# Narrow projection groups chained in PSUM, other terms for the wide ones, and weights and gate stores on other queues

## The chip, the cores and the metric

The kernel runs on one core of a Trainium2 chip as one launch. The metric is the device time of that launch in microseconds (us); the time before is the median of 3 runs.

## What is computed

One decoder layer on 2048 tokens of width 1024, in float32:

```
n    = RMSNorm(x)
proj = n @ w_in                      # split into gq, gk, gv, gr, glow, dq, dk, dv
o_a  = gated linear attention(gq, gk, gv, log_sigmoid(glow @ w2 + b) / 16)
o_a  = RMSNorm(o_a) * silu(gr)
o_b  = dilated sliding-window attention(dq, dk, dv), three branches, relative bias
h    = x + [o_a ; o_b] @ w_out
y    = RMSNorm(h + square(relu(RMSNorm(h) @ w_ff1)) @ w_ff2)
```

## The kernel before

**Stages.** The input projection takes the first 460 us, attention and the output projection follow to about 1040 us, then the first feed-forward product (FF1, to about 1690 us) and the second (FF2). Every large product is done by a Strassen-Winograd scheme of seven products instead of eight. Each factor is split into a high and a low part of 32 bits, and a product is three matmuls per piece (mm3, L139 to L142: L140 high by high, L141 low by high, L142 high by low). TensorE (PE) does nothing but these, transposes and the attention products.

**The projection.** The columns of w_in are nine groups (L249): dv, gr, dq, dk, dq, dk, gq, gk, gv. Two passes over the two halves of the tokens make 18 groups, g = 0 to 17. dv and gv are 256 columns wide on each of two sides n, gr 264 (the last 16 of its 512 + 16 are the low-rank gate); these are the wide groups. The other twelve are narrow, 128 columns a side. A group is seven products j in the order 1, 2, 5, 6, 3, 4, 7, one entry each of a list (jobs, L254). In a narrow product the combined weights stand in PE and 512 tokens stream past, twelve matmuls for the product; in a wide one the tokens stand and four token tiles take twelve matmuls each.

**What a product needs and leaves.** Two jobs ahead (L751), prep (L278) makes a product's weights: ScalarE (ACT) writes the high part wcomb (L288), VectorE (DVE) the low part (L290, or L292 with a scale for dq and gq), and DVE updates the sums of weights in place in the raw weights wraw (L294 to L300). Raw weights of the next group come from w_in by four loads (L271) on the queue of SyncE (SP), each issued when its quarter is free. A product's result stands in a bank of PSUM; the names ps_a, ps_c, ps_o, ps_d are kinds of bank, 2, 3, 1 and 2 of them, and bank() takes them in the turn a, c, a, o. rest() (L440 to L458) empties a bank: ACT copies products 1, 5 and 4 (L440, L445, L453), DVE adds products 2, 6, 3 and 7 (L442, L447, L450, L455) and adds three more times in SBUF (L448, L458 twice). So each group has seven DVE additions of results. The results stand in five halves of three slots called acc; c12 and c22 change places from group to group (L323).

**What is done with results.** finish (L329) sends them to DRAM: dq and dk are split again into high (L341, ACT) and low (L342, DVE) and stored by SP (L343). The gate group gr passes through log_sigmoid (L205 to L208), an exponential (L353), a product on DVE (L354), one on GpSimd (POOL, L355) and a store to srD by SP (L356); its last columns go to gate (L308), which transposes them (L315), multiplies them on PE (L318) and stores log gates to glD (L321, SP).

**FF1.** product1 (L1439) keeps its seven products in the order 1, 2, 6, 5, 7, 3, 4: products 1, 6, 7 and 4 go on accumulating in one bank, 5 and 3 in another, with a copy or an addition taken out between them. The weights w1raw come by GpSimd's queue (L1387), a group at a time in two halves, one for each half k of the rows.

**Order.** A list scheduler with a simulated timeline orders every engine's instructions when the kernel is built; the order of code is only its starting point. PSUM banks and SBUF slots are waited for by semaphores that the framework sets.

The functions that the diff touches:

Of the kernel before, what the change touches and what calls it, by code (L numbers as in the profile page):

```python
# [31 lines left out]
OTHER = [7, 9, 10, 11, 12, 13] + [14 * k + n for k in (1, 2, 3) for n in (0, 6, 10, 11, 12, 13)]  # L32
# [82 lines left out]
def emit(tc, a, stop=99):  # L115
# [137 lines left out]
    order = (1, 2, 5, 6, 3, 4, 7)  # L253
    jobs = [(g, j) for g in range(2 * NG) for j in order]  # L254
    w_in = a["w_in"].rearrange("o (c p) n -> p (o c) n", p=128)
    raws = [view(slot("wraw"), (2, 4, 264)) for _ in range(2)]
# [9 lines left out]

    def load_w(g, n, k):

        if g < 2 * NG:
            _, c0, w = groups[g % NG]  # L270
            SP.dma_start(raws[n][:, k, :, :w], w_in[:, 4 * k:4 * k + 4, c0 + n * w:c0 + n * w + w])  # L271
# [6 lines left out]
    def prep(at):  # L278
# [5 lines left out]
        (a11, a12), (a21, a22) = [[raws[n][:, k, :, :w] for k in range(2)] for n in range(2)]  # L284
        hi, lo = comb(at, w)
        src = {1: a11, 2: a12, 5: a21, 6: a21, 3: a12, 4: a22, 7: a21}[j]
# [8 lines left out]
        if j == 5:  # L295
            V.tensor_tensor(a21, a21, a11, op=OP.subtract)
            load_w(g + 1, 0, 0)
            V.tensor_tensor(a12, a12, a21, op=OP.subtract)
        if j == 6:
            V.tensor_tensor(a21, a22, a21, op=OP.subtract)  # L300
        if j == 3:
            load_w(g + 1, 0, 1)
        if j == 4:
            load_w(g + 1, 1, 1)
        if j == 7:
            load_w(g + 1, 1, 0)

    def gate(glow, t):  # L308
# [7 lines left out]
        V.tensor_copy(gT[:50], pt[:50, :128])  # L316
        pg = ps("d")[:, :256]
# [5 lines left out]
    def outputs(g):  # L323

        if g == 0:
            return c11, c12, c21, CX
        return (c11, (c12, c22)[g % 2], c21, (c22, c12)[g % 2])

    def finish(g, n, k, i):  # L329
# [4 lines left out]
        if w == 128:  # L334
# [5 lines left out]
            hi = c[:, 512:1024].bitcast(FR)  # L340
            A.activation(hi, c[:, :512], AF.Copy)  # L341
            V.tensor_tensor(c[:, :512], c[:, :512], hi.bitcast(F32), op=OP.subtract)  # L342
# [5 lines left out]
        if kind == "gr":  # L348
# [7 lines left out]
            SP.dma_start(srD[tk, j:j + m], s[:, :m])  # L356
# [11 lines left out]
    banks, held, late = [0], {}, []  # L368
# [31 lines left out]
    def product(at, i):  # L400
# [6 lines left out]
        if e == 0:  # L407
            held[j, i] = bank()
        p = held[j, i - e]
        B, W = TB[j], comb(at, w)  # L410
        n = w
        if w == 128:
            n = 512
            for c in range(4):
                mm3(p, W[0][:, c], W[1][:, c], B[0][:, c], B[1][:, c], c == 0, c == 3)
# [6 lines left out]
        def rest():  # L422
# [11 lines left out]
            def done(*which):  # L434
                for t in range(i - e, i + 1):
                    for n, k in which:
                        finish(g, n, k, t)

            if j == 1:
# [6 lines left out]
            elif j == 6:  # L446
                V.tensor_tensor(ix, q, ix, op=OP.add)  # L447
                V.tensor_tensor(c12, X, c22, op=OP.add)  # L448
            elif j == 3:
                V.tensor_tensor(i12, q, i12, op=OP.add)  # L450
                done((0, 1))
            elif j == 4:
                A.activation(i21, q, AF.Copy)  # L453
            else:
                V.tensor_tensor(ix, q, ix, op=OP.add)  # L455

                def sums(v, which, keep=lambda ins: None):
                    keep(V.tensor_tensor(v, v, X, op=OP.add))  # L458
                    done(which)

                for v, which in ((c21, (1, 0)), (c22, (1, 1))):
                    if at == len(jobs) - 1 and i == 3:
                        late.append((sums, v, which))
                    else:
                        sums(v, which)
# [3 lines left out]
    def bias_rows():  # L469

        rb, oh, rbo = xp[:33, :8], view(xp[:33, 8:], (3, 384)), view(bp[:8], (3, 384))
        SP.dma_start(rb[:32], a["rel_bias"])
        V.memset(rb[32:33], NEG)
        V.tensor_scalar(rb[:32], rb[:32], -1.0, None, op0=OP.mult)
        SP.dma_start(oh, a["c_onehot"])
        for d in range(3):
            p = ps("o")
            T.matmul(p[:8, :384], rb, oh[:, d], start=True, stop=True)
            V.tensor_copy(rbo[:, d], p[:8, :384])
        SP.dma_start(rowD, rbo)  # L480

# [14 lines left out]
    X = {}  # L496
# [1363 lines left out]
```

## Time and profile before

| | |
|---|---|
| runs | 2239.35, 2244.89, 2244.66 us, median 2244.66 |
| profiled execution | 2242.91 us, its span 2241.1 us (1.8 us lie around it) |
| PE busy | 2212.8 us (99%), 12420 matmuls |
| DVE busy | 1680.8 us (75%), 3173 instructions |
| ACT busy | 1253.5 us (56%), 2506 instructions |
| POOL busy | 533.6 us (24%), 535 instructions |

PE leaves 28.3 us of the span idle. A matmul's record runs on past the start of the next one, so PE's busy time is the union of records that overlap. Idle time of another engine costs nothing by itself.

### The profile page before, as it was taken

How to read it: one execution, taken by the hardware profiler on the slowest of the kernel's cores; microseconds unless marked ns; L12 is line 12 of the kernel's file. 1: busy time of each engine (PE TensorE's matmuls, PEld its weight loads, DVE VectorE, ACT ScalarE, POOL GpSimd, SP SyncE). 2: the span in 40 equal slices, each digit the busy share in tenths (PEclk: the TensorE clock that was granted, in tenths of full speed). 3: DMA queues.
4: the chain of work that ended last, by engine and by line, in shares of the span. 5: the costliest groups of instructions: out<-in, count | busy, mean ns of one | idle time of the engine just before them, and what ended most of it. 6: DMA issues, size and time to landing. Idle time of an engine off the chain costs nothing.

```text
span 2241.1 us, 35330 instructions
## 1 busy us (share of the span) xinstructions
PE 2212.8 (99%) x12420; PEld 1918.8 (86%) x12420; DVE 1680.8 (75%) x3173; ACT 1253.5 (56%) x2506; POOL 533.6 (24%) x535
## 2 busy tenths in 40 slices
PE   9999999999999999999999999999999999999998
PEld 8978998799999998887888888888888888888877
DVE  8787868666677677778777788777685697576798
ACT  7675446435787785555655566555555433333446
POOL 1110001016577673000000000000006222031462
PEclk9999999999999999999999999999999999999999
DMA  6467854787977877767744456555489988677775
GB/s 214 141 188 229 256 165 121 213 250 251 312 256 222 271 214 241 247 225 249 220 141 149 140 177 199 165 167 167 130 279 287 306 282 276 216 250 253 250 258 197
DMA packets 340934, 491.79 MB, mean 219 GB/s; under 512 B 20503, under 2 KB 237162, under 8 KB 330004
## 3 DMA queue, kind: packets, MB, share of 16 engines
q1 hardware_dynamic: 319842, 394.88, 54.6%
q0 software_dynamic: 13568, 41.95, 7.6%
q10 hardware_dynamic: 7346, 52.70, 6.3%
q8 instruction: 98, 1.61, 0.3%
q14 instruction: 80, 0.66, 0.1%
HBM read 335.52 MB, written 158.66 MB: 221 GB/s over the span
## 4 chain that ended last, share of the span: by engine, by line
PE 68%; issue 16%; DVE 7%; DMA 5%; POOL 2%; ACT 1%; SPq 0%; POOLq 0%; ACTq 0%; DVEq 0%
PE ps_a L141 7%; PE ps_a L142 6%; PE ps_a L140 6%; PE ps_c L141 5%; PE ps_c L142 5%; PE ps_c L140 5%; PE ps_a L909 4%; PE ps_d L141 3%; PE ps_d L142 3%; PE ps_d L140 3%; PE ps_o L141 3%; PE ps_o L140 3%; PE ps_o L142 3%; PE ps_d L890 3%; PE ps_c L872 2%
## 5 line engine op out<-in xcount | busy, mean ns | idle before, releaser
L490 ACT ACTIVATE cb<-bs 128x1024 fp32r<-128x1024 f32 x104 | 110.1, 1059 | 287.9 <-PE ps_o L141 94.6
L491 DVE TENSOR_TENSOR cb<-bs,cb 128x1024 fp32r<-128x1024 f32 x104 | 157.9, 1519 | 137.7 <-ACT cb L490 137.4
L1680 POOL TENSOR_TENSOR bs<-bs,rb 128x1024 f32<-128x1024 f32 x60 | 174.3, 2912 | 318.1 <-DMA bs<-w_ff 282.4
L491 DVE TENSOR_TENSOR w1comb<-w1raw,w1comb 128x512 fp32r<-128x512 f32 x224 | 153.2, 686 | 94.0 <-ACT w1comb L490 93.9
L1387 POOL DMA_DIRECT2D w1raw<-w_ff x64 | 48.2, 754 | 702.6 <-DVE w1comb L491 532.8
L490 ACT ACTIVATE w1comb<-w1raw 128x512 fp32r<-128x512 f32 x224 | 139.9, 627 | 92.0 <-PE ps_c L142 27.2
L881 ACT ACTIVATE pe<-pe,O 128x256 f32<-128x256 f32 (+1 forms) x384 | 157.5, 454 | 45.6 <-DVE O L880 41.9
L909 PE MATMUL ps_a<-v,pt 128*128 128x65 f32 x1200 | 180.8, 253 | 1.5 <-DVE pt L899 1.4
L909 PEld LDWEIGHTS ps_a<-v,pt 128*128 128x128 f32 x1200 | 175.7, 195 | 2.9 <-DVE pt L899 1.7
L880 DVE CUSTOM_DVE_ANT_0 pe<-ps_c,nb 128x256 f32<-128x256 f32 (+1 forms) x384 | 126.7, 360 | 46.8 <-PE ps_d L890 16.5
L890 PE MATMUL ps_d<-ident,pe 128*128 128x128 f32 x600 | 160.5, 281 | 0.0
L288 ACT ACTIVATE wcomb<-wraw 128x512 fp32r<-128x512 f32 (+2 forms) x119 | 90.1, 757 | 99.2 <-PE ps_a L141 33.0
L140 PE MATMUL ps_c<-hb,w1comb 128*128 128x512 f32 x320 | 124.6, 390 | 0.0
L141 PE MATMUL ps_c<-hb,w1comb 128*128 128x512 f32 x320 | 124.4, 389 | 0.0
L142 PE MATMUL ps_c<-hb,w1comb 128*128 128x512 f32 x320 | 124.1, 389 | 0.0
L491 DVE TENSOR_TENSOR ca<-ra,ca 128x1024 fp32r<-128x1024 f32 x84 | 121.8, 1451 | 0.1
L141 PE MATMUL ps_c<-cb,ca 128*128 128x512 f32 x312 | 121.5, 389 | 0.0
L140 PE MATMUL ps_c<-cb,ca 128*128 128x512 f32 x312 | 121.5, 389 | 0.0
L142 PE MATMUL ps_c<-cb,ca 128*128 128x512 f32 x312 | 121.4, 389 | 0.0
L890 PEld LDWEIGHTS ps_d<-ident,pe 128*128 128x128 f32 x600 | 109.2, 186 | 0.3
L355 POOL TENSOR_TENSOR acc<-acc,misc 128x264 f32<-128x264 f32 (+1 forms) x32 | 29.4, 924 | 319.3 <-DVE acc L354 303.9
L140 PE MATMUL ps_a<-wcomb,tb 128*128 128x256 f32 (+1 forms) x344 | 97.7, 284 | 0.0
(476 smaller groups left out, 7248.8 us busy)
## 6 DMA issues: line engine op xcount, KB each, us to landing
ra<-actD ACTq DMA_DIRECT2D x50, 1024.0 KB, 7.3
actD<-ring SPq DMA_DIRECT2D x176, 256.0 KB, 3.1
rb<-w_ff SPq DMA_DIRECT2D x88, 512.0 KB, 5.3
bs<-w_ff SPq DMA_DIRECT2D x72, 512.0 KB, 6.0
w1raw<-w_ff POOLq DMA_DIRECT2D x64, 512.0 KB, 5.3
k<-kD SPq DMA_DIRECT2D x16, 1024.0 KB, 7.9
rb<-hTD SPq DMA_DIRECT2D x28, 512.0 KB, 5.8
wraw<-w_in SPq DMA_DIRECT2D x48, 256.0 KB, 3.6
```

What stands on the lines that cost most here:

```text
L140: T.matmul(out, sh, mh, start=first, stop=False, **kw)
L141: T.matmul(out, sl, mh, start=False, stop=False, **kw)
L142: T.matmul(out, sh, ml, start=False, stop=last, **kw)
L288: A.activation(hi, src, AF.Copy, scale=sc)
L490: A.activation(hi, src, AF.Copy)
L491: V.tensor_tensor(lo, src, hi.bitcast(F32), op=OP.subtract)
L880: V.tensor_tensor_reduce(p, s, bias, scale=1.0, scalar=BIG, op0=OP.add, op1=OP.min, accum_out=nm)
L881: A.activation(p, p, AF.Exp, bias=nm, scale=-1.0)
L890: T.transpose(pb[:, i * 128:i * 128 + 128], src, ident)
L909: T.matmul(self.b.opsum[:, n % 4], self.pt[:, i * 128:i * 128 + 128], self.b.v[:, blk, cols], start=first, stop=last)
L1387: G.dma_start(raw1[g % 2][:, 4 * k:4 * k + 4], w1[:, 4 * k:4 * k + 4, g0:g0 + 256])
L1680: (engines or ((G,), (V, V))[len(sums) - 1])[e].tensor_tensor(v, v, r, op=OP.add if op == "+" else OP.subtract)
```

## The change

**Narrow groups** take the order of FF1. Products 1, 6, 7 and 4 accumulate in one bank ps_a, 5 and 3 in one of ps_o or ps_c by turns, 2 in ps_c. ACT copies products 1, 6 and 5 out, DVE adds for 2, 7 and 3, and the last product of dq and dk is split into high and low straight from the bank. That is three DVE additions a group in place of seven. Their raw weights stand in halves of the slots, so that the next group's loads are issued some seven jobs ahead (table FREE).

**Wide groups** take the order 1, 2, 5, 6, 3, 7, 4 and add other terms, so that no copy of product 4 is needed. The last finishing step of gr, (1, 0), is put off and done one token tile after each of the next four jobs (behind). **Queues:** the raw weights of wide groups and the gate stores to srD are issued by GpSimd. gate is cut in two, and its matmul (gate_product) comes one product later. **FF1:** the second group's weights come in four quarters. A few steps move by a job or two (OTHER, bias_rows).

```diff
-    order = (1, 2, 5, 6, 3, 4, 7)
-    jobs = [(g, j) for g in range(2 * NG) for j in order]
+    order, linked = (1, 2, 5, 6, 3, 7, 4), (1, 2, 6, 5, 7, 3, 4)
+    chained = lambda g: groups[g % NG][2] == 128
+    jobs = [(g, j) for g in range(2 * NG) for j in (linked if chained(g) else order)]
...
+    def raw_of(g, n):
+        w = groups[g % NG][2]
+        if w > 128:
+            return raws[n][:, :, :, :w]
+        return view(raw_slots[n][:, GP * (g % NG % 2):], (2, 4, 128))
...
-            SP.dma_start(raws[n][:, k, :, :w], w_in[:, 4 * k:4 * k + 4, c0 + n * w:c0 + n * w + w])
+            (SP if g < 2 or chained(g) else G).dma_start(raw_of(g, n)[:, k], w_in[:, 4 * k:4 * k + 4, c0 + n * w:c0 + n * w + w])
...
+        if chained(g):
+            if j == 2:
+                V.tensor_tensor(a11, a21, a11, op=OP.subtract)
+                V.tensor_tensor(a12, a12, a11, op=OP.subtract)
+            if j == 6:
+                V.tensor_tensor(a11, a22, a11, op=OP.subtract)
...
+        for n, k in FREE[g][j]:
+            load_w(g + 1, n, k)
+
+    FREE = {}
+    for g in range(2 * NG):
+        if not chained(g):
+            FREE[g] = {5: [(0, 0)], 3: [(0, 1)], 4: [(1, 1)], 7: [(1, 0)]}
+            if chained(g + 1):
+                FREE[g] = {5: [(0, 0), (0, 1)], 7: [(1, 0), (1, 1)]}
+        elif chained(g + 1):
+            FREE[g] = {1: [(0, 0)], 2: [(0, 1)], 6: [(1, 1)], 5: [(1, 0)]}
+        else:
+            FREE[g] = {1: [(0, 0)], 2: [(1, 0)], 3: [(0, 1)], 4: [(1, 1)]}
...
-            hi = c[:, 512:1024].bitcast(FR)
-            A.activation(hi, c[:, :512], AF.Copy)
-            V.tensor_tensor(c[:, :512], c[:, :512], hi.bitcast(F32), op=OP.subtract)
+            lo, hi = c[:, :512], c[:, 512:1024].bitcast(FR)
+            if q is None:
+                q = lo
+            elif kind == "dq":
+                lo, hi = [by_rows(v) for v in (lo, hi)]
+            A.activation(hi, q, AF.Copy)
+            V.tensor_tensor(lo, q, hi.bitcast(F32), op=OP.subtract)
...
-            SP.dma_start(srD[tk, j:j + m], s[:, :m])
+            G.dma_start(srD[tk, j:j + m], s[:, :m])
...
-        if e == 0:
-            held[j, i] = bank()
-        p = held[j, i - e]
+        root = {6: 1, 7: 1, 4: 1, 3: 5}.get(j, j) if chained(g) else j
+        if e == 0 and root == j:
+            held[j, i] = ps({1: "a", 2: "c", 5: "oc"[g % 2]}[j]) if chained(g) else bank()
+        p = held[root, i - e]
...
+            if chained(g):
+                if j in (1, 6):
+                    A.activation(ix, q, AF.Copy)
+                elif j == 5:
+                    A.activation(i22, q, AF.Copy)
+                elif j == 4 and kind in ("dq", "dk"):
+                    done((1, 0), q=q)
+                elif j == 4:
+                    A.activation(i21, q, AF.Copy)
+                    done((1, 0))
+                else:
+                    v, y, of = {2: (i11, ix, (0, 0)), 7: (i22, i22, (1, 1)), 3: (i12, ix, (0, 1))}[j]
+                    V.tensor_tensor(v, q, y, op=OP.add)
+                    done(of)
...
+                V.tensor_tensor(i21, q, i21, op=OP.add)
+                if kind == "gr":
+                    behind.append((done, (1, 0)))
+                else:
+                    done((1, 0))
...
+            ready = gated[:]
             product(at, i)()
+            for t in ready:
+                gate_product(t)
+                gated.remove(t)
+        if behind and chained(g):
+            f, *args = behind.pop(0)
+            f(*args)
...
-            for k in halves:
-                G.dma_start(raw1[g % 2][:, 4 * k:4 * k + 4], w1[:, 4 * k:4 * k + 4, g0:g0 + 256])
+            for n in range(2) if g == 1 else (None,):
+                cs = slice(0, 256) if n is None else slice(128 * n, 128 * n + 128)
+                for k in halves:
+                    G.dma_start(raw1[g % 2][:, 4 * k:4 * k + 4, cs], w1[:, 4 * k:4 * k + 4, g0:g0 + 256][:, :, cs])
```

Lines of the changed kernel are numbered anew: L283 is the weight load, L303 the high part, L305 and L307 the low part, L356 the store to glD, L345 and L353 the gate's matmuls, L382 to L384 the split and the store of dq and dk, L395 to L397 gr's two products and its store to srD, L484 to L494 the emptying of narrow banks.

**First place: SP's queue in the second pass, where the gate group gr gives way to dq.** Rows are stores of the gate (srD, glD), loads of weights (wraw), dq's store (qD) and spreads of the bias (rbD). Before:

```order
L271 DMA wraw<-w_in 128x4x128
L356 DMA srD<-acc 128x248 x2
L271 DMA wraw<-w_in 128x4x128
L343 DMA qD_86<-acc 256x1x512
L321 DMA glD<-acc 128x256
L486 DMA rbD_111<-rowD 128x2x384
L271 DMA wraw<-w_in 128x4x128
L356 DMA srD<-acc 128x248
```

And in the changed kernel:

```order
L283 DMA wraw<-w_in 128x4x128 x2
L541 DMA rbD_111<-rowD 128x2x384
L283 DMA wraw<-w_in 128x4x128 x6
L356 DMA glD<-acc 128x256
L283 DMA wraw<-w_in 128x4x128 x2
L384 DMA qD_86<-acc 256x1x512
L356 DMA glD<-acc 128x256
```

The loads stood singly between stores of gr, which wait for GpSimd's product; now eight stand ahead of the first glD store, and no srD store stands on this queue.

**Second place: DVE in the first pass, where the first dq group gives way to dk.** acc_116, acc_117 and acc_118 are the three result slots, wcomb and wraw weights, xp_114 the rows of x for the second pass. Before, dq's last two splits (L342) stand ahead of the addition for dk's product 2 (L442):

```order
L313 TENSOR_TENSOR small_113<-acc_117,small_113 128x16
L342 TENSOR_TENSOR acc_117<-acc_117 128x512
L342 TENSOR_TENSOR acc_118<-acc_118 128x512
L298 TENSOR_TENSOR wraw_119<-wraw_119,wraw_120 128x4x128
L442 TENSOR_TENSOR acc_116<-ps_c_1682,acc_116 128x512
```

In the changed kernel ps_a_1439 is the chained bank of dq, ps_a_1648 that of dk:

```order
L395 TENSOR_TENSOR acc_117<-acc_118,acc_117 128x248
L305 TENSOR_TENSOR wcomb_123<-wraw_119,wcomb_123 128x4x128
L208 SCALAR_TENSOR_TENSOR acc_118<-ps_d_1488,acc_118 128x256
L619 SCALAR_TENSOR_TENSOR xp_114<-xp_114,stats_80,misc_112 128x1024
L305 TENSOR_TENSOR wcomb_121<-wraw_120,wcomb_121 128x4x128
L383 TENSOR_TENSOR acc_117<-ps_a_1439,acc_117 128x4x16x8
L494 TENSOR_TENSOR acc_117<-ps_a_1648,acc_117 128x512
```

Now the last tile of gr is still being finished there (L395, then POOL's product and the store); behind it stands dq's last split (L383), and directly behind that the addition for dk's product 7 (L494).

**Third place: PE in the first pass, at the first dq group.** The number behind a bank tells which use of it is meant; tb1, tb5 and tb6 are the tokens of products 1, 5 and 6. Before, product 6 follows product 5 and has a bank of its own:

```order
L141 MATMUL ps_o_1559<-tb5_128,wcomb_122 128x512
L142 MATMUL ps_o_1559<-tb5_129,wcomb_122 128x512
L140 MATMUL ps_a_1576<-tb6_130,wcomb_123 128x512
L141 MATMUL ps_a_1576<-tb6_130,wcomb_123 128x512
L142 MATMUL ps_a_1576<-tb6_131,wcomb_123 128x512
```

In the changed kernel:

```order
L141 MATMUL ps_a_1439<-tb1_124,wcomb_123 128x512
L142 MATMUL ps_a_1439<-tb1_125,wcomb_123 128x512
L345 MATMUL ps_d_1310<-ident_67,misc_112 50x128
L353 MATMUL ps_d_1313<-misc_112 128x256
L140 MATMUL ps_a_1439<-tb6_130,wcomb_122 128x512
L141 MATMUL ps_a_1439<-tb6_130,wcomb_122 128x512
L142 MATMUL ps_a_1439<-tb6_131,wcomb_122 128x512
```

The scheduler has put product 2 ahead of product 1 here, so product 6 follows product 1 on the same bank with two gate matmuls between them. In the second pass five matmuls of product 2 stand there as well.

87 lines of the change are left out of this document (44 added, 43 removed).

## The prediction

> **What bounds the kernel now.** I read the page's busy times first.
>
> ```profile
> span 2241.1 us, 35330 instructions
> PE 2212.8 (99%) x12420; PEld 1918.8 (86%) x12420; DVE 1680.8 (75%) x3173; ACT 1253.5 (56%) x2506; POOL 533.6 (24%) x535
> ```
>
> PE is busy for all but 28.3 us of 2241.1. The change leaves PE's matmuls as many as they were, so it can give back only waits, late starts and lowered clock, and only where its edits reach: the projection and the start of FF1. The same times by stretches (columns: width, busy time of PE, its weight loads, DVE, ACT and POOL, then PE's clock, the share of DMA and GB/s) show where those lie.
>
> ```profile
> 110.00:180.00 70.00, 68.38 (x311) 54.87 (x310) 62.97 (x115) 49.26 (x112) 6.76 (x8) 1.00 0.62 192
> 360.00:430.00 70.00, 66.86 (x290) 53.48 (x289) 54.67 (x103) 42.17 (x94) 6.60 (x7) 0.98 0.63 189
> 200.00:300.00 100.00, 100.00 (x707) 93.20 (x706) 78.68 (x96) 47.01 (x65) 0.00 (x0) 1.00 0.74 234
> 399.60:403.60 4.00, 3.38 (x9) 2.57 (x10) 2.85 (x5) 3.34 (x8) 0.00 (x0) 0.62 0.51 146
> ```
>
> The first two stretches hold, one in each pass, the passage from gr to dq and dk. PE idles 1.62 us in the first and 3.14 us in the second; the stretch between them is full. The last row is a part of the second: there the clock fell to 0.62 of full speed, which loses 0.38 x 4.00 = 1.5 us more that no idle time shows. Now the waits of the projection (what PE waited for, total us, times, longest).
>
> ```profile
> PE ps_a L140 <- ACT acc L445: 2.0, 1, 2.0
> PE ps_a L141 <- DVE wcomb L292: 0.8, 2, 0.5
> PE ps_o L141 <- DVE wcomb L290: 0.7, 1, 0.7
> PE ps_c L141 <- DVE wcomb L290: 0.6, 1, 0.6
> PE ps_a L140 <- ACT wcomb L288: 0.3, 1, 0.3
> PE ps_o L140 <- ACT wcomb L288: 0.3, 1, 0.3
> ```
>
> One is for a bank that ACT had not emptied, six are for weights. These seven waits add to 4.7 us. A matmul's record lasts 0.39 us while the next starts 0.23 us after it (the rows at 396.79 and 397.01 below), so each wait hides another 0.16 us: 1.1 us in seven. The loss of the two passages is 1.62 + 3.14 + 1.5 + 1.1 = 7.4 us. Why the work came late is in the timelines and in the waits of SP's queue.
>
> ```profile
> 391.79 0.52 SPq L343 DMA_DIRECT2D qD<-acc  x1
> 396.79 0.39 PE L141 MATMUL ps_c<-tb,wcomb 128*128 128x512 f32 x1
> 397.01 0.39 PE L142 MATMUL ps_c<-tb,wcomb 128*128 128x512 f32 x1
> 397.92 0.28 PE L318 MATMUL ps_d<-misc 128*128 128x256 f32 x1
> 399.57 0.60 ACT L445 ACTIVATE acc<-ps_a 128x512 f32<-128x512 f32 x1 [5.65 <-DMA qD<-acc]
> 400.22 0.56 PE L140 MATMUL ps_a<-tb,wcomb 128*128 128x512 f32 x1 [2.02 <-ACT acc L445]
> 377.47 0.69 DVE L294 TENSOR_TENSOR wraw<-wraw 128x512 f32<-128x512 f32 x1 [2.74 <-DMA wraw<-w_in]
> ...
> SPq L356 <- POOL acc L355: 57.4, 29, 6.1
> SPq L271 <- DVE wraw L296: 27.6, 11, 7.7
> ```
>
> ACT's copy waited 5.65 us for a store of q, issued at 391.79, to leave the half that the copy overwrites; PE waited behind it. DVE waited 2.74 us for weights. SP, which issues both in order, stood 57.4 us at gr's stores for GpSimd's product: late issue is behind both.
>
> **The projection's edits.** First, the removal. In the first order listing the loads no longer stand between srD stores, and eight of them stand ahead of the first glD store, so the 57.4 us on SP disappear from their path. Narrow weights are loaded some seven jobs ahead; a product takes 2.72 us, by the twelve matmuls between these two rows:
>
> ```profile
> 1038.07 0.39 PE L140 MATMUL ps_d<-wo,mcomb 128*128 128x512 f32 x1
> 1040.79 0.39 PE L140 MATMUL ps_a<-hb,w1comb 128*128 128x512 f32 x1
> ...
> wraw<-w_in SPq DMA_DIRECT2D x48, 256.0 KB, 3.6
> L458 DVE TENSOR_TENSOR acc<-acc 128x512 f32<-128x512 f32 x28 | 18.1, 684 | 0.0
> L288 ACT ACTIVATE wcomb<-wraw 128x512 fp32r<-128x512 f32 x79 | 49.5, 627 | 33.7 <-PE ps_a L142 9.9 <-DVE wraw L294 6.3 <-PE ps_c L142 5.4
> 156.47 1.07 ACT L440 ACTIVATE acc<-ps_o 128x512 f32<-128x512 f32 x1
> ```
>
> Seven products are 19 us against a landing of 3.6 us, so the six weight waits and ACT's wait for the store, whose half is now rewritten six or seven products after its issue, should go: I take all 7.4 us. Twelve groups lose four DVE additions each, 48 x 0.684 = 33 us of DVE work. I count them at nothing, since in the full stretch above DVE works 78.68 of 100 us without holding PE; they are cover for what follows. If that cover is used up by late work, its price is in the rivals.
>
> Next, the additions. Chaining makes a product wait until the one before on its bank has been taken out. Products 1 to 6, 6 to 7 (with 5 between), 5 to 3 (with 7 between) and 7 to 4 (with 3 between) are four hand-overs in each of twelve groups, 48 in all. Where one product lies between, 2.72 us must hold a plain copy of 0.60 (row at 399.57) or dq's strided one of 1.07, with a 0.63 us weight copy ahead of it. FF1 does the same today:
>
> ```profile
> PE ps_d L141 <- DVE w1comb L491: 0.2, 1, 0.2
> 1120.00:1600.00 480.00, 479.75 (x2116) 396.50 (x2115) 363.60 (x723) 278.26 (x469) 38.20 (x51) 1.00 0.53 162
> L1470 ACT ACTIVATE xs<-ps_a 128x512 f32<-128x512 f32 x16 | 9.4, 588 | 2.2 <-PE ps_a L142 2.2
> ```
>
> In 480 us of it PE waits once, 0.2 us, and that for weights, with 0.588 us copies. So the hand-overs cost nothing in the middle of a pass. The exception is the third order listing: the first pass has two gate matmuls between product 1 and product 6, not a product. The copy takes 1.07 us and its hand-overs about 0.3 (a short wait behind ACT below is 0.34); the two gate matmuls give about 0.25 back (the larger is the record of 0.28 at 397.92, of which a part overlaps). That is **1.1 us** lost in the first pass; in the second the five matmuls of product 2, 1.13 us, cover it. From below, the copy could be hidden altogether (0); from above it is 1.07 + 0.63 behind a weight copy + 0.3 = 2.0.
>
> The deferred finish of gr, now stored by GpSimd, is what I know least. In the second listing dq's last split (L383) must wait for gr's store to leave acc_117, and directly behind it stands the addition of dk's product 7, on which dk's product 4 waits. From product 7's end to product 4's start lies one product: 2.72 less 0.68 for each of the two and 0.34 for the hand-over leaves about 1.0 us. The nearest rows for the store are the same transfer issued by SP, and GpSimd's issues for FF1:
>
> ```profile
> 158.31 0.50 PE L140 MATMUL ps_a<-tb,wcomb 128*128 128x512 f32 x1 [0.34 <-ACT wcomb L288]
> srD<-acc SPq DMA_DIRECT2D x16, 124.0 KB, 1.7
> L355 POOL TENSOR_TENSOR acc<-acc,misc x32: 718/833/1713, 79.2 to 380.4; 128x264 f32<-128x264 f32 x16, 128x248 f32<-128x248 f32 x16
> L1387 POOL DMA_DIRECT2D w1raw<-w_ff x64: 748/748/987, 1025.4 to 1617.0; - x64
> DMA to landing us min/median/max: 4.2/5.3/10.0
> ```
>
> The transfer decides more than the queue does: 124 KB landed in 1.7 us, the 512 KB of GpSimd's in 5.3. If the deferred store lands in 1.7 us, nothing is late; in 5.3, 5.3 - 1.7 - 1.0 = 2.6 us a pass; in 10.0, 7.3 us a pass. I take **0.5 us** for both passes, nearest the first row with the longer issue (0.75 against SP's 0.52 at 391.79), and keep 0 and 14.6 as ends. The wide loads on GpSimd's queue are 16 issues of 0.75 us on an engine that is 24% busy and have at least one product, 2.72 us or more, to hide behind; with that cover gone they would show as waits for wraw.
>
> On that queue the page "SBUF — State Buffer" of the Trainium skill, section "Who interferes with whom", says that DVE's copies and casts in a 2-port mode lock GpSimd out and so starve the descriptors it makes, and that a DVE operation with two SBUF inputs holds up a GpSimd operation that reads SBUF. By that rule the change puts its stores on the wrong queue, and the third rival comes true. The trace speaks mostly against it: FF1's 64 issues took 748 to 987 ns beside a DVE that is 75% busy, though POOL's product did stretch from 718 to 1713 ns.
>
> **FF1's second weights.**
>
> ```profile
> 1038.54 1.50 POOL L1387 DMA_DIRECT2D w1raw<-w_ff  x2 [11.35 <-PE ps_a L142]
> 1046.81 0.63 ACT L490 ACTIVATE w1comb<-w1raw 128x512 fp32r<-128x512 f32 x1 [6.37 <-DMA w1raw<-w_ff]
> 1047.49 0.50 PE L140 MATMUL ps_d<-hb,w1comb 128*128 128x512 f32 x1 [2.48 <-ACT w1comb L490]
> w1raw<-w_ff POOLq DMA_DIRECT2D x64, 512.0 KB, 5.3
> ```
>
> PE waits 2.48 us (with the hidden 0.16, 2.64) for 512 KB issued at 1038.54. The first use needs one quarter, 256 KB. Such loads land in 3.6 us (wraw) against 5.3 for 512 KB (w1raw): **1.7 us** earlier, so 1.7 saved. The ends are 0, if all four quarters share the transfer engines and land together, and the full 2.64.
>
> **The sum.** 7.4 + 1.7 - 1.1 - 0.5 = 7.5 us. The profiled execution took 2242.9 us (2241.1 of span and 1.8 around it), so **2235.4, say 2235 us**. The median of the runs, 2244.7, lies 1.8 us above that execution and the lowest run, 2239.35, 3.6 below. About 0.3%, 6.7 us, is what a measurement of this kernel can tell from no change; the forecast lies just beyond it, 9.7 under the median. With the good ends the gain is 7.4 + 2.6 = 10.0, so 2232.9, or 2229 with a run as low as the lowest.
>
> One part of the 7.4 is the lowered clock, which I put down to the 2.02 us wait just ahead of it. The page "TensorE: Matmul & The Clock Gate" of the Trainium skill, section "What's actually happening", has the clock halved only after an idle window of some 3.4 us. By its wording a 2-us wait is too short, the 1.5 us would have another cause and might stay: an estimate of 2236.9. The trace has the low clock right after the wait, 0.62 over 4 us; but the 2.48 us wait at 1047.49 shows no such fall (the stretch of 1000 to 1100 has clock 1.00), so it is not certain either way:
>
> ```profile
> 1000.00:1100.00 100.00, 95.23 (x449) 78.50 (x448) 79.71 (x118) 61.40 (x111) 6.25 (x8) 1.00 0.76 244
> ```
>
> **Rivals.** *Waits replaced in kind.* The deferred stores land in 5.3 us and each pass stalls 2.6 us at dk's product 4, with 1.5 us of low clock behind it: 2 x 4.1 - 0.5 = 7.7 back, 2243.1, no change. For it speaks that ACT and DVE are fuller at this passage (62.97 of 70 us) than elsewhere; against it, that a 124-KB store took 1.7 us.
>
> *Slower by tight banks.* The 48 hand-overs have one product where ACT and DVE had about three. If three DVE operations of 0.684 stand ahead of an addition of 0.684, they fill 2.74 us and PE misses its start. At 0.34 us a time, the shortest wait shown, 48 cost 16.3: 2251.7. It decides as soon as the taking out begins 2 us after a product's end; ahead of dq's strided copies that is less far off than in FF1. Against it stands FF1's one wait in 480 us, and that DVE has four operations a group fewer.
>
> *Slower by GpSimd's queue.* Stores and loads issued there are held up, and the deferred store lands after 10.0 us: 7.3 + 1.5 of clock a pass, 17.6 - 0.5 = 17.1 back, 2252.5. For it is the 10.0 row; against it the steady 748 ns of issue.
>
> **How the numbers follow.** My forecast (2231 to 2238) 0.50; waits in kind (2238 to 2247) 0.33; tight banks 0.11; GpSimd's queue 0.06. So faster by over 0.3% has 0.50, within 0.3% 0.33, slower 0.17. The range leaves out the far ends of the slower cases: 2229 to 2249.
>
> **What would show it.** Right: the waits of the projection no longer name acc or wcomb for more than 1 us, the clock is 1.00 through both passages, one wait of about 1 us behind L484 stands in the first pass, SP no longer waits for POOL, and FF1's second product waits under 1 us. Wrong: many waits of 0.3 us behind L484 or L494, a wait behind L494 at dk's fourth product with a landing of srD over 3 us, or waits for wraw in gr, dv and gv.

## The result

The changed kernel takes 2246.70 us in the median of 16 runs, the kernel before 2239.89 us in 16 runs beside them. The ratio is 1.0025, 95% interval 1.0016 to 1.0034: slower by about 5.6 us (the two medians alone lie 6.8 apart), where 2235 us and a gain were forecast. (The three runs shown before the prediction lay high; the profiled execution of 2242.9 us, against which the sum was made, is 3 us above the median of 16.)

The profile of the changed kernel comes from an execution of 2246.55 us. First its page:

```profile
span 2244.8 us, 35289 instructions
PE 2214.1 (99%) x12420; PEld 1922.3 (86%) x12420; DVE 1645.8 (73%) x3125; ACT 1251.3 (56%) x2496; POOL 565.2 (25%) x585
```

DVE lost 35 us of work, as many as were counted (33), and PE has the same 12420 matmuls. The work went; the time did not come. By stretches (width, busy PE, weight loads, DVE, ACT, POOL, clock, DMA share, GB/s), the changed kernel and then the one before:

```profile
60.00:140.00 80.00, 76.97 (x507) 70.58 (x506) 61.73 (x118) 52.50 (x129) 19.92 (x27) 0.96 0.47 144
140.00:360.00 220.00, 220.00 (x1465) 201.65 (x1464) 162.32 (x235) 113.75 (x209) 24.75 (x35) 1.00 0.66 202
360.00:460.00 100.00, 95.80 (x423) 77.44 (x423) 68.78 (x122) 55.13 (x115) 14.03 (x18) 1.00 0.67 203
1040.00:1120.00 80.00, 75.60 (x338) 60.88 (x337) 65.22 (x107) 48.58 (x85) 7.48 (x10) 1.00 0.73 232
```

```profile
60.00:140.00 80.00, 79.31 (x536) 72.90 (x535) 68.13 (x126) 58.73 (x144) 15.49 (x16) 1.00 0.45 137
140.00:360.00 220.00, 218.99 (x1452) 198.87 (x1451) 170.80 (x254) 111.44 (x205) 7.29 (x10) 1.00 0.65 202
360.00:460.00 100.00, 96.84 (x421) 77.95 (x420) 75.21 (x135) 54.48 (x115) 6.60 (x7) 0.98 0.69 201
1040.00:1120.00 80.00, 76.52 (x347) 62.62 (x346) 66.16 (x111) 47.81 (x84) 5.27 (x8) 1.00 0.75 232
```

The middle of the passes is full now, a gain of 1.0 us. The first stretch lost: 3.03 us idle in place of 0.69, and the clock at 0.96. The third idles 4.20 us in place of 3.16, without the lowered clock. FF1's first stretch idles 4.40 in place of 3.48. What PE waits for in the projection is almost all new:

```profile
PE ps_d L353 <- DVE acc L208: 2.4, 2, 1.8
PE ps_d L345 <- DVE acc L208: 1.9, 1, 1.9
PE ps_c L141 <- DVE wcomb L305: 1.3, 1, 1.3
PE ps_a L140 <- ACT acc L484: 0.8, 1, 0.8
PE ps_d L345 <- DVE misc L346: 0.4, 1, 0.4
PE ps_a L140 <- DVE acc L511: 0.4, 1, 0.4
```

Of the old waits only one for weights is left, and no row of SP's waits names gr's stores; SP now stands 33.7 us at the stores of log gates (L356) behind DVE's L208. That last wait for weights, 1.3 us at 425 us, stands behind a load that is still late for DVE:

```profile
423.44 0.69 DVE L309 TENSOR_TENSOR wraw<-wraw 128x512 f32<-128x512 f32 x1 [4.50 <-DMA wraw<-w_in]
```

New are waits of the gate's own matmuls (L345, L353) for a bank that DVE's L208 has not read, and one for ACT's copy out of the chained bank. In the first pass they stand so in the timeline, PE, ACT and DVE in that order; in brackets the idle time before the row and what ended it:

```profile
115.15 0.39 PE L353 MATMUL ps_d<-misc 128*128 128x256 f32 x1 [1.85 <-DVE acc L208]
116.36 0.80 PE L140 MATMUL ps_a<-tb,wcomb 128*128 128x512 f32 x1 [0.82 <-ACT acc L484]
...
111.90 0.41 ACT L205 ACTIVATE acc<-acc 128x248 f32<-128x248 f32 x1 [1.88 <-DVE acc L395]
115.28 1.03 ACT L484 ACTIVATE acc<-ps_a 128x512 f32<-128x512 f32 x1
...
114.68 0.41 DVE L208 SCALAR_TENSOR_TENSOR acc<-ps_d,acc 128x256 f32<-128x256 f32 x1
```

The stretches around it, in the columns used above:

```profile
117.00:123.00 6.00, 6.00 (x17) 4.58 (x16) 2.44 (x6) 2.56 (x6) 0.83 (x2) 0.53 0.71 222
104.00:117.00 13.00, 10.33 (x58) 8.58 (x57) 12.99 (x31) 8.05 (x24) 7.27 (x11) 0.95 0.58 190
```

DVE works 12.99 of the 13 us up to 117: it is full, mostly with the last tiles of gr. ACT stands idle 1.88 us for DVE, and so copies dq's product 1 out at 115.28, behind gr's steps. PE stands 2.67 us and then runs at 0.53 of its clock for 6 us, which loses another 2.8; from 113 to 117 us the mean clock was 0.84, which loses another 0.6. In the kernel before, DVE was as full in the same 13 us, and PE was busy throughout:

```profile
104.00:117.00 13.00, 13.00 (x73) 11.12 (x72) 12.88 (x33) 10.53 (x30) 4.13 (x5) 1.00 0.53 170
```

In the second pass the wait has another end. POOL, ACT, DVE and PE of the changed kernel:

```profile
392.75 0.57 POOL L397 DMA_DIRECT2D srD<-acc  x1 [0.30 <-POOL acc L396]
397.61 1.03 ACT L382 ACTIVATE acc<-ps_a 128x512 fp32r<-128x512 f32 x1 [3.87 <-DMA srD<-acc]
398.67 1.02 DVE L383 TENSOR_TENSOR acc<-ps_a,acc 128x512 f32<-128x512 f32 x1 [4.48 <-ACT acc L382]
400.08 0.29 PE L345 MATMUL ps_d<-ident,small 128*50 128x128 f32 x1 [1.90 <-DVE acc L208]
```

The deferred store of gr's last tile is issued at 392.75; it lands 4.8 us later, and from 392.75 to 397.60 the transfer engines are 0.93 busy. ACT waits 3.87 us for it, DVE behind ACT, and PE's gate matmul behind DVE.

### The profile page after: what moved, and what is told of

The parts are those of the page before. It is cut to its first block, busy times and chain, and to the rows that moved or that the text cites. A ratio compares the mean times of both kernels' runs of the same rounds, so it can differ in the third digit from the quotient of the medians.

```text
span 2244.8 us, 35289 instructions
## 1 busy us (share of the span) xinstructions
PE 2214.1 (99%) x12420; PEld 1922.3 (86%) x12420; DVE 1645.8 (73%) x3125; ACT 1251.3 (56%) x2496; POOL 565.2 (25%) x585
## 4 chain that ended last, share of the span: by engine, by line
PE 70%; issue 14%; DVE 7%; DMA 5%; POOL 2%; ACT 1%; SPq 1%; POOLq 0%; DVEq 0%; ACTq 0%
PE ps_a L141 7%; PE ps_a L140 7%; PE ps_a L142 7%; PE ps_c L141 6%; PE ps_c L140 6%; PE ps_c L142 6%; PE ps_a L971 4%; PE ps_d L141 3%; PE ps_d L142 3%; PE ps_d L140 3%; PE ps_d L952 3%; PE ps_o L140 3%; PE ps_o L141 3%; PE ps_o L142 3%; PE ps_c L934 2%
## 5 line engine op out<-in xcount | busy, mean ns | idle before, releaser
L303 ACT ACTIVATE wcomb<-wraw 128x512 fp32r<-128x512 f32 (+2 forms) x119 | 90.0, 757 | 89.0 <-PE ps_a L141 38.7
L305 DVE TENSOR_TENSOR wcomb<-wraw,wcomb 128x512 fp32r<-128x512 f32 (+2 forms) x77 | 74.9, 973 | 42.4 <-ACT wcomb L303 42.3
L1522 ACT ACTIVATE acc<-acc 128x512 f32<-128x512 f32 x96 | 60.6, 632 | 71.2 <-DVE acc L1541 31.4
```

The costliest lines, as they stand in the source:

```text
L303: A.activation(hi, src, AF.Copy, scale=sc)
L305: V.tensor_tensor(lo, src, hi.bitcast(F32), op=OP.subtract)
```

## The experiments

As a sum for each part I use late starts: for every matmul the time from its start to the next one's, less the median of its line and form, added up where it is over 0.06 us more. They hold idle time, hidden waits and low clock. For the projection (60 to 560 us) and for FF1 (1040 to 1640 us), beside the timed ratio to runs of the kernel before that were made with it:

| kernel | ratio, 95% interval | projection | FF1 |
|---|---|---|---|
| before | 1 | 13.3 us | 5.4 us |
| changed | 1.0025 (1.0016 to 1.0034) | 17.0 | 8.0 |
| e1, gr's stores on SP | 1.0030 (1.0018 to 1.0042) | 18.0 | 7.7 |
| e2, gate whole | 1.0017 (1.0007 to 1.0028) | 15.8 | 6.0 |
| e3, no deferral | 1.0011 (1.0000 to 1.0021) | 13.5 | 6.9 |
| e4, halves | 1.0027 (1.0015 to 1.0039) | 19.2 | 5.7 |
| e5, product 2 pinned | 1.0043 (1.0031 to 1.0056) | 22.7 | 9.4 |
| e6, before + quarters | 1.0005 (0.9997 to 1.0013) | 12.5 | 6.0 |
| e8 = e2 + e3 + e4 | 0.9997 (0.9987 to 1.0008) | 13.2 | 9.7 |
| e9 = e8, first dq unchained | 0.9978 (0.9968 to 0.9988) | 10.8 | 4.9 |
| e10 = e8, old wide terms | 1.0037 (1.0023 to 1.0051) | 21.6 | 5.7 |
| e11 = e8, all on SP | 0.9996 (0.9984 to 1.0007) | 17.9 | 6.1 |
| e12 = e3, first dq unchained | 1.0009 (1.0000 to 1.0019) | 13.5 | 8.4 |
| e13 = e9, gate split | 1.0000 (0.9990 to 1.0009) | 13.4 | 3.7 |
| e14 = e9, quarters | 0.9996 (0.9987 to 1.0006) | 12.1 | 7.9 |

Late starts are of one execution each; 0.001 of the ratio is 2.2 us. With intervals of some 0.001 to either side, two rows of the table that differ by less than about 0.0014 (3 us) are not clear of noise.

**e1: gr's stores on SP's queue again.**

```diff
-            G.dma_start(srD[tk, j:j + m], s[:, :m])
+            SP.dma_start(srD[tk, j:j + m], s[:, :m])
```

> The changed kernel with gr's stores to srD issued by SP again. Theory A (PE, in order, waits at the gate's own matmuls for a ps_d bank that DVE's L208 frees late): the waits of PE for L208 in the first pass (1.85 us at 113.0, then 0.82 and some 3 us of half clock) stay as they are, and the time stays within 1.5 us of the changed kernel's. Theory B (gr's deferred stores land late on GpSimd's queue and hold ACT's L382, and behind it DVE and PE): ACT's wait of 3.87 us for srD in the second pass falls under 1 us, PE's 1.90 us wait there goes, and the time falls by 2 to 4 us. Against both: SP waits for GpSimd's product again, weights come late, and the time rises by 2 us or more.

The time stayed. The wait for the store stayed too, SP and then ACT:

```profile
392.26 0.58 SPq L397 DMA_DIRECT2D srD<-acc  x1
399.43 1.02 ACT L382 ACTIVATE acc<-ps_a 128x512 fp32r<-128x512 f32 x1 [5.03 <-DMA srD<-acc]
```

7.2 us from issue to ACT's start, with SP as the issuer: GpSimd's queue is not what makes it late. The late moment of the store and the transfers around it remain as reasons, untested (the engines are 0.91 busy from 388 to 400 us here). PE stands behind ACT again, now 3.7 us for the weights that ACT writes after its split; the waits of the first pass stay at 1.7 and 0.8 us, as theory A had it. So theory B is right on the store and wrong on GpSimd. The page "SBUF — State Buffer" of the Trainium skill, section "Who interferes with whom", would have GpSimd's descriptors starved beside DVE's 2-port modes; no run here shows that.

**e2: the gate whole again.**

```diff
-        gated.append(t)
+        gate_product(t)
```

> The changed kernel with the gate in one piece again: its product is issued behind its own transpose, not one product later. Theory A with the split as its cause: the waits of PE for L208 (4.3 us in all) fall under 1 us, the half clock of the first pass goes with them, and the time falls by 5 to 7 us, to the kernel of before or under it. Rival (the split only moves the wait: PE waits for the gate's transpose to be copied instead): PE's waits at L345 and L353 together stay at 3 to 5 us and the time within 1.5 us of the changed kernel's.

Between the two expectations: 1.8 us less, which is not clear of noise. PE's waits, longest first:

```profile
PE ps_a L140 <- ACT acc L484: 2.5, 3, 1.4
PE ps_d L353 <- DVE misc L346: 1.7, 1, 1.7
PE ps_d L345 <- DVE acc L208: 1.4, 2, 1.0
```

They are as long as in the changed kernel, 5.6 us, and have only moved: to the copy of the transpose (L346) and to ACT's copy out of the chained bank. That is the rival's account.

**e3: no deferred finish.**

```diff
-                if kind == "gr":
-                    behind.append((done, (1, 0)))
-                else:
-                    done((1, 0))
+                done((1, 0))
```

> The changed kernel with gr's last finishing step done at once, not one tile after each of the next four jobs. Theory B: srD is stored before dq needs the slot, ACT's L382 no longer waits for it (3.87 us before), PE's wait at the second pass goes, 2 to 4 us less. Theory A: the first pass is where DVE works without a gap at gr's end; four more tiles there make it longer, PE's waits for L208 rise by 1 us or more, and the time stays or rises by up to 3 us.

3 us less, at the edge of noise; e1 and e4, which keep the deferral, lie at 1.0030 and 1.0027. ACT's wait for srD falls from 3.87 to 0.4 us in the second pass, and PE's 1.9 us wait behind it goes. In the projection stand, among others:

```profile
PE ps_d L353 <- DVE acc L208: 2.3, 2, 1.8
PE ps_a L140 <- ACT acc L484: 1.1, 1, 1.1
```

The longest of the first row, 1.8 us, is the first pass's, which stays; the second row is a new wait in the second pass, at the end of gr.

**e4: FF1's weights in halves again.**

```diff
-            for n in range(2) if g == 1 else (None,):
+            for n in (None,):
```

> The changed kernel with FF1's second weights in two halves again. If the quarters are worth what the wait for them lost (2.48 us before, 1.23 us in the changed kernel), the time rises by 1.2 us. If the new waits of FF1 behind them (PE for xh 0.97, for acc L1537 0.71 and 0.44) come with the quarters, these go and the time falls by about 1 us. Both theories of the projection expect nothing there.

No change in the time. In its profile FF1 lost 2.3 us less, while the store of the second pass, which the edit does not touch, landed later: POOL and ACT

```profile
393.42 0.57 POOL L397 DMA_DIRECT2D srD<-acc  x1 [0.30 <-POOL acc L396]
401.60 1.02 ACT L382 ACTIVATE acc<-ps_a 128x512 fp32r<-128x512 f32 x1 [7.51 <-DMA srD<-acc]
```

so PE's wait behind the deferred store was 1.9 us in the changed kernel's profile and 5.5 in this one.

**e5: product 2 pinned between products 1 and 6 in the first dq group.**

```diff
+                    pin=g == 2 and j == 2 and c == 0, skip_group_check=True)
...
+        if pin:
+            tc.keep_in_program_order(ins)
```

> The changed kernel with one matmul tied to the order of the code: the first of product 2 in the first dq group (g = 2), so that product 2 stands between products 1 and 6 on PE. Theory C (the first pass loses because product 6 follows product 1 at once on a bank that ACT empties late): PE's 0.82 us wait for L484 goes, 2.7 us of work stand there, and of the 6.1 us that the first pass loses from 113 to 123 us (waits of 1.85 and 0.82, then half clock) at least 3 go; the time falls by 2 to 4 us. Theory D (DVE and ACT are behind with gr's last tiles, so the first wait on PE's way shows it wherever it stands): the wait of 1.85 us for L208 stays, product 6 waits again or a gate matmul does, the first pass's loss stays within 1.5 us, and the time too.

The time rose by 4 us, which neither theory had. The 0.82 us wait for the chained bank went from its place. The projection's waits (lines are 2 higher here):

```profile
PE ps_d L347 <- DVE acc L210: 4.9, 1, 4.9
PE ps_d L355 <- DVE acc L210: 2.0, 2, 1.4
PE ps_a L140 <- ACT acc L486: 1.4, 1, 1.4
PE ps_a L140 <- DVE acc L496: 1.2, 1, 1.2
```

The first row is the deferred store again, at 407 us in the second pass, which the pin does not name; it landed 7.6 us after its issue. In the first pass waits of 1.4, 1.0 and 0.9 us stand between 105 and 130 us and no lowered clock, so that from 113 to 123 us PE loses 2.4 us in place of some 6: that much is as theory C had it. But two waits at chained banks (1.2 and 1.4 us) came at 135 and 143 us, where the changed kernel has none, and the time did not fall. So the adjacency is not worth the 2 to 4 us of theory C, and most of the rise in this profile belongs to the store; the run doesn't show more than that.

**e6: the kernel before with quarters alone** (the hunk of the diff on FF1).

> The kernel before with FF1's second weights in quarters and nothing else. Theory of the prediction: PE's wait of 2.48 us for w1comb at 1044 falls by 1.2 to 1.7 us, and the time by as much. Rival, from the changed kernel's trace (waits for xh of 0.97 and for acc of 0.71 and 0.44 behind it, which went with the halves): the wait falls, two others of 2 us in sum come, and the time is the same within 1 us or 1 us more.

The rival's account: no gain. PE's waits in FF1, where before only 3.5 for w1comb (longest 2.5) and 0.2 stood:

```profile
PE ps_d L140 <- ACT w1comb L490: 2.4, 3, 1.4
PE ps_a L140 <- DVE acc L1478: 0.9, 1, 0.9
PE ps_a L140 <- DVE xh L1548: 0.8, 1, 0.8
```

The changed kernel shows why (POOL, ACT, DVE, PE):

```profile
1040.92 2.98 POOL L1448 DMA_DIRECT2D w1raw<-w_ff  x4 [11.60 <-PE ps_a L142]
1047.96 0.63 ACT L545 ACTIVATE w1comb<-w1raw 128x512 fp32r<-128x512 f32 x1 [4.96 <-DMA w1raw<-w_ff]
1052.21 0.69 DVE L1463 TENSOR_TENSOR w1raw<-w1raw 128x512 f32<-128x512 f32 x1 [1.10 <-DMA w1raw<-w_ff]
1065.31 0.50 PE L140 MATMUL ps_a<-hb,w1comb 128*128 128x512 f32 x1 [0.97 <-DVE xh L1607]
```

Four issues took 2.98 us where two took 1.50. The first quarter was there 7.0 us after its issue, where the half took 8.3; a later one was late and stopped DVE 1.10 us. DVE is busy for all of the 13 us from 1053 to 1066, so it cannot catch up, and its additions to xh and acc come late in turn.

**e7: the changed kernel with the wide groups' old order and terms.** It makes log gates of half the tokens from other tokens, since two tiles share a buffer before the split gate's product; the amount of work is the same.

```diff
-    order, linked = (1, 2, 5, 6, 3, 7, 4), (1, 2, 6, 5, 7, 3, 4)
+    order, linked = (1, 2, 5, 6, 3, 4, 7), (1, 2, 6, 5, 7, 3, 4)
...
-                V.tensor_tensor(c22, X, c22, op=OP.add)
+                V.tensor_tensor(c12, X, c22, op=OP.add)
...
+                V.tensor_tensor(ix, q, ix, op=OP.add)
+                for v, which in ((c21, (1, 0)), (c22, (1, 1))):
+                    V.tensor_tensor(v, v, X, op=OP.add)
+                    done(which)
...
```

> The changed kernel with the wide groups' old order (1, 2, 5, 6, 3, 4, 7), old terms and no deferred finish; narrow chaining, loads ahead, GpSimd's queue, the split gate and the quarters stay. If the wide groups' new terms pile up gr's tail, the first pass's loss of 7.5 us (60 to 140 us) falls under 4, and ACT's wait for srD in the second pass goes: 4 to 6 us less than the changed kernel, so about the kernel of before. Theory D: gr's tail comes even later, with both last results behind product 7; chained dq needs ACT at once, and the first pass loses as much or up to 3 us more; only the second pass's 2 to 3 us go.

The ratio was 1.0052 (1.0039 to 1.0065): slower still, by 6 us, which neither account had: the late starts in the projection fell a little (15.4 us from 17.0), and those of FF1 doubled (15.8 from 8.0). e10 makes the same edit on e8.

**e8: deferral, split gate and quarters undone together.**

> The changed kernel without the deferred finish, with the gate in one piece and with FF1's halves. If the three parts add as they did one by one (deferral about 3 us, whole gate 1.5, quarters 0 to 1), the time lies 4 to 5 us under the changed kernel's and 1 to 2 above the kernel of before. If what is left (chained narrow groups, new terms of the wide ones, earlier loads) is a gain that the three parts hid, it lies 2 us or more under the kernel of before.

Back to the kernel before (0.9997), no worse than the sum of the parts. PE's waits in the projection still name the gate and the chained bank:

```profile
PE ps_a L140 <- ACT acc L484: 2.8, 3, 1.7
```

The gate's two rows, 1.7 and 1.4 us, are the same as in e2. So the three parts together hold the whole loss: 6.3 us lie between the changed kernel and e8. The longest of the waits for L484 stands in the first pass behind one of gr's stores, though no finish is deferred here (ACT, PE):

```profile
139.21 1.06 ACT L382 ACTIVATE acc<-ps_a 128x512 fp32r<-128x512 f32 x1 [4.17 <-DMA srD<-acc]
143.11 0.50 PE L140 MATMUL ps_a<-tb,wcomb 128*128 128x512 f32 x1 [1.68 <-ACT acc L484]
```

**e9: e8 with the first dq group unchained.**

```diff
-    chained = lambda g: groups[g % NG][2] == 128
+    chained = lambda g: groups[g % NG][2] == 128 and g % NG != 2
...
-            (SP if g < 2 or chained(g) else G).dma_start(raw_of(g, n)[:, k], ...)
+            (SP if g < 2 or w == 128 else G).dma_start(raw_of(g, n)[:, k], ...)
```

The second line keeps that group's loads on SP's queue.

> The kernel of the run before (no deferred finish, gate in one piece, halves) with the first dq group behind gr unchained: its seven products have banks of their own, in the wide groups' order and with their terms; the other ten narrow groups stay chained. Theory E (what the change loses in the projection is that a chained group stands right behind gr, whose tail keeps ACT and DVE busy, so PE waits at once for a bank or a gate behind them): PE's waits for L484 of 2.8 us and most of the gate's 3.1 us go, the projection's late starts fall from 13 us to 8 or less, and the time falls by 3 to 5 us, 1 to 3 us under the kernel of before. Rival (the tail of gr alone does it, chained or not): the waits of the gate stay, the projection's late starts stay at 11 us or more, and the time within 1.5 us of the kernel of before.

On the time theory E holds and more: 0.9978, 5 us under the kernel before, 4.3 under e8 and 10.5 under the changed one. The waits for L484 and the gate fall from 5.9 us to 1.6. But the projection's late starts are 10.8 us, nearer the rival's 11 than the 8 expected, and a wait of 2.1 us for weights came in the second pass. The waits of the projection:

```profile
PE ps_c L141 <- DVE wcomb L305: 2.4, 2, 2.1
PE ps_a L140 <- ACT acc L484: 1.0, 1, 1.0
PE ps_d L345 <- DVE acc L208: 0.6, 1, 0.6
```

And its stretch at gr's end:

```profile
104.00:117.00 13.00, 12.51 (x72) 10.62 (x70) 12.08 (x32) 10.08 (x30) 8.03 (x12) 1.00 0.66 213
```

DVE is nearly as full up to 117 us, but PE is now 12.51 busy of 13 (11.42 in e8). Unchaining takes away two things at once: the copies that must be prompt behind gr, and ACT's wait for gr's store at dq's split, of which e9 has none. No run separates them. Nor does a run have the early loads and the new terms without any chaining, so it is not shown that chaining the other ten groups pays. Not all of the 5 us lie in the projection: its late starts are 2.4 to 2.7 us fewer than those of e8, e12 and e13, and FF1's are also low.

**e10: e8 with the wide groups' old order and terms** (the edit of e7).

> The same kernel without the three parts, and with the wide groups' old order and terms as well; all narrow groups chained. If the new terms of the wide groups are what fills DVE at gr's end, PE's waits between 100 and 125 us and at 365 us fall by half and the time by 2 us or more against the kernel of before. Theory E: gr's last two results now both come behind its last product, next to the chained dq, so PE's waits for L484 stay or grow, and the time is the same as without this edit or up to 3 us longer.

Theory E's side, and dearer than it said: 9 us over e8. One row of its projection tells it:

```profile
PE ps_a L140 <- ACT acc L484: 8.4, 5, 3.6
```

So with all narrow groups chained the new terms of the wide ones are needed: without them PE waits 8.4 us for copies out of the chained bank.

**e11: e8 with wide weights and gr's stores on SP's queue.**

```diff
-            (SP if g < 2 or chained(g) else G).dma_start(raw_of(g, n)[:, k], ...)
+            SP.dma_start(raw_of(g, n)[:, k], ...)
-            G.dma_start(srD[tk, j:j + m], s[:, :m])
+            SP.dma_start(srD[tk, j:j + m], s[:, :m])
```

> The same kernel without the three parts, and with gr's stores and the wide weights on SP's queue again, so that GpSimd's queue carries neither. If GpSimd's queue is worth what the waits of SP's loads say, weights come late at gr's end (PE waits for wcomb of 1 us or more, as in the kernel of before) and the time rises by 1 to 3 us. If the queue matters little because the loads are issued seven jobs ahead, the time stays within 1 us.

The same time (0.9996 against e8's 0.9997). What GpSimd's queue costs or saves is less than the 3 us that these runs can tell. (Its one profile has more late starts in the projection, 17.9 us, and fewer in FF1; the timed runs do not bear that out.)

**e12: the changed kernel with two edits, no deferral and the first dq group unchained.**

> The changed kernel with two edits: no deferred finish of gr, and the first dq group unchained; the gate in two pieces and FF1's quarters stay. If these two places are the loss (theories B and E), the time lies within 2 us of the kernel with all four edits, 3 us or more under the kernel of before and 8 or more under the changed kernel. If the split gate and the quarters cost what they did one by one (some 1.5 and up to 1 us), it lies 2 to 3 us above the kernel with all four, near the kernel of before.

Past the second expectation: 3.6 us better than the changed kernel, but 7 worse than e9, and 2 above the kernel before. Against e3 (1.0011) unchaining the first dq group changed nothing here (1.0009), so its gain shows only with the gate whole and the halves. No wait for L484 is left, but weights come late by DVE, and FF1 lost 8.4 us. Which of the two remaining parts does it was tried one at a time on e9.

**e13: e9 with the split gate. e14: e9 with the quarters.** The edits are those of e2 and e4 put back.

> The best kernel (no deferred finish, first dq group unchained, gate whole, halves) with the gate in two pieces again. If the gate in two is the cost, the projection's late starts rise from 10.8 to 13 us or more and the time by 3 us or more, to the kernel of before; FF1's stay under 6 us. If it is the quarters, the time stays within 1.5 us of the best kernel's.

> The best kernel with FF1's second weights in quarters again. If the quarters are the cost, FF1's late starts rise from 4.9 to 8 us (a shorter wait for w1comb, with waits for xh of 1.0 and for acc of 0.9 in its place) and the time by 3 us or more. If they cost what they did in the kernel of before, 1 us or less, the gate in two is the larger cost.

Each alone loses what e9 had won, 4.9 us and 4.0 us. e13's late starts rose by 2.6 us in the projection, e14's by 3.0 in FF1 and 1.3 in the projection. e12 has both and lies 2 to 3 us above either, so whether the two costs add is not clear of noise.

## Why the prediction was wrong

**Where the miss lies.** The sum gave 7.5 us less, the runs 5.6 us more. The deferral, the gate in two pieces and the quarters stood in the sum with 0.5 us lost, nothing, and 1.7 us gained; undoing them together takes 6.3 us back (e8), so they hold the whole loss. The rest, the removal less the exception, stood there as a gain of 6.3 us and is worth nothing in e8; 5 us of it come when the group behind gr is unchained (e9). What failed is the price of the new order where gr ends: the steps below say which term had it wrong.

**The removal, 7.4 us.** The mechanism was right: all loads but one come in time, SP no longer stands at gr's stores, the wait for the store of q is gone, and of the seven waits one for weights is left (1.3 us for wcomb at 425 us). The old waits went; others came in their places.

**The covers.** "I count them at nothing ... they are cover for what follows" is the step that failed. The 33 us of DVE additions went, but not from gr's end in the first pass: there DVE was full before (12.88 of 13 us) and is full now (12.99). I took the fullness of the stretch from 200 to 300 us for a measure of slack, and that of FF1, where nothing like gr's tail exists. The chain needs ACT and DVE promptly, and does so first right behind the tile work that keeps them behind. Before, product 1 of dq had a bank of its own and its copy could be late.

**The exception, 1.1 us.** The 0.82 us for the copy came, at the place named. But ahead of it stood 1.85 us for the gate, which was not in the sum at all, and around and behind it stood 3.4 us of low clock (0.6 and 2.8): some 6 us in place of 1.1. Taking away the adjacency of products 1 and 6, which I made its cause, won no time (e5). That the backlog behind gr is the cause is what the rows show in the first pass and what e9 speaks for; e12 shows no gain from the same edit, so it stays in part argued. The gate in two pieces, which I gave no term, cost 4.9 us on e9 (e13); the 1.8 us in the changed kernel (e2) are not clear of noise.

**The deferred store, 0.5 us.** The dependence was the one I described, but ACT's half of the split (L382) waited, not DVE's, and PE stood at the gate's transpose (L345), not at dk's product 4, with 1.9 us in the changed kernel's profile and 5.5 in e4's. To stay "nearest the first row" was the wrong choice: 1.7 us is the median of stores of which many were issued where the transfer engines were half busy (0.51 from 105 to 130 us). The profile's list of transfers from 390 to 400 us would have told: there the kernel before kept the 16 engines full (0.98 from 388 to 400 us), and stores of 128 KB (last column, median us to landing) took

```profile
glD<-acc SPq DMA_DIRECT2D x2, 128.0 KB, 8.3
```

8.3 us; the deferred store then took 4.8. Undoing the deferral gave 3 us (e3).

**The quarters, 1.7 us.** The wait for w1comb fell from 2.48 to 1.23 us, 1.25 saved, near the term. What I did not ask is who waits for the other three quarters: DVE, and 2.1 us of waits for xh and acc came behind (0.97, 0.7 and 0.4 in the changed kernel). Alone the quarters gained nothing (e6), and on e9 they lost 4 us (e14).

**The rivals.** In time the result lies between the first (no change) and the second (9 us slower). Waits replaced in kind came nearest in mechanism: a landing of 4.8 us against its 5.3 and a wait of 1.9 us against its 2.6, though in one pass only. Of tight banks one wait of 0.8 us at a chained bank came, not 48 of 0.34; the others at gr's ends are the gate's. Slower through GpSimd's queue did not come (e1, e11).

What stays open: why e13 and e14 lose 4 to 5 us each while their profiled spans (2240.6 and 2240.7 us) lie only 1.4 and 1.5 over e9's 2239.2. Part of it is that e9's profiled execution, 2240.95 us, is near the slowest of its nine (2236.60 to 2241.08, median 2239.36), while theirs are at their medians (2242.4). e9 was timed in one series, apart from theirs. The scheduler orders everything behind an edit anew, and FF2's late starts, which no edit is about, range from 1.8 to 6.4 us in these profiles, so a single profile does not settle a microsecond.

## What to carry to other kernels

Chaining products in one bank turns an eviction that may be late into one that must be prompt, so look for the busiest stretch of the engines that evict, not their mean, and try the group right behind it unchained (4.3 us from e8 to e9). The 33 us freed on DVE were no cover here, since DVE stayed full at gr's end. Read a transfer's landing from the stretch it will stand in, and when a load is cut in pieces ask who waits for the last piece.

## What the hardware showed beyond that

The clock of PE fell after some waits of about two us and not after others: 0.62 over 4 us after 2.02 us (before, second pass), 0.84 over 4 us with waits of 1.85 and 0.82 in them and 0.53 over the next 6 (changed, first pass), no fall after 1.90 (changed, second pass) nor after 2.48 (before, FF1). The page "TensorE: Matmul & The Clock Gate" of the Trainium skill, section "What's actually happening", asks for an idle window of about 3.4 us; here shorter waits sufficed, some of the time, so a wait's price carries a chance of 1.5 to 3.4 us on top.
